# The mLSTM's norm factors and output scaling on GpSimd instead of VectorE and ScalarE, in a hybrid mLSTM and differential-attention block

## The chip, the cores and the metric

The kernel runs on one core of a Trainium2 chip. The metric is the device time of one execution in microseconds (us), given as the median of several runs. One further execution is recorded by the hardware profiler; all views quoted here come from it. The core's engines work side by side, each taking its own queue of instructions in order: TensorE (PE in the profile; PEld is its weight load), VectorE (DVE), ScalarE (ACT), GpSimd (POOL) and SyncE (SP, which here mostly issues DMAs).

## What is computed

One layer over a sequence of 1024 tokens with a model width of 1024, all in fp32. The input is normalised and projected by `w_in`; one part goes through a bidirectional mLSTM with 4 heads of 256 channels, another through differential attention with 8 heads; both branches are gated, mixed and projected out. The change touches the end of the mLSTM branch, the RMS norm of each head's output:

```python
def rmsnorm(x, g):
    xf = x.astype(jnp.float32)
    y = xf * lax.rsqrt(jnp.mean(xf * xf, axis=-1, keepdims=True) + NORM_EPS)
    return (y * g.astype(jnp.float32)).astype(x.dtype)
...
h_fw = mlstm_one_direction(mq, mk, mv, i_fw, lf_fw)
h_bw = flip(mlstm_one_direction(flip(mq), flip(mk), flip(mv), flip(i_bw), flip(lf_bw)))
hm = rmsnorm((h_fw + h_bw).transpose(0, 2, 1, 3), ml_norm_g[layer])
hm = hm.reshape(B, S, ML_WIDTH).astype(x.dtype)
y_a = hm * jax.nn.sigmoid(a_o) * jax.nn.silu(a_z)
```

For each token and head there is one norm factor, `rsqrt(mean(h*h) + eps)`, and the 256 outputs of that token and head are multiplied by it.

## The kernel before

The kernel passes through stages one after the other: normalising and transposing the input, projections and convolutions, differential attention (about 460 to 1110 us of the span), the mLSTM (about 1145 to 1390 us), then the mixing of the branches and the output projection. Large products are split in a high and a low part (`H`, `L`) and computed as three fp32r products each. The high part is a cast on ScalarE, the low part a subtraction on VectorE or GpSimd.

The order of TensorE's instructions is written out by hand after the opening stage (`keep(E.PE)`, the `Weaver`, and `ml_units` for the mLSTM). For ScalarE, VectorE, GpSimd and SP, the framework's planner makes the order of each queue at compile time, from the program's order and its own estimate of durations: of the instructions that it holds to be ready, it takes the one that stands first in the program. On the chip every queue is then taken strictly in that order, and an instruction that waits holds up those behind it.

The mLSTM runs head by head, n = 0 to 3, in `ml_units` (L1239 on). A head's sequence is cut in 8 tiles of 128 tokens, `tt` = 0 to 7. The steps of a tile, all in `ml_head`:

- `scores` (S): TensorE makes the 256-wide score tile; for both directions GpSimd masks the decay terms (`affine_select`, L1136, output `W`), ScalarE takes the exponential (L1138), VectorE multiplies with the scores and sums (L1139).
- `t_tile` (I): TensorE multiplies with the running states; VectorE makes the denominators and their reciprocal `rr` (L1165 to L1174), ScalarE writes the first part of the output `hm` (L1179) and scales `W` (L1183), VectorE adds the second direction (L1185, L1188).
- `transposes` (T): TensorE transposes `W`, ScalarE casts it to `WH` (L1198), VectorE makes `WL`.
- `pv` (P): TensorE multiplies `W` with the values into `PO`; VectorE adds that to `hm` (L1209); ScalarE squares it and sums along the row into one column of `ssq` (L1210). After the last tile (`tt == 7`), the norm factors of the whole head, 128x8 numbers `rs`, come from `self.rsqrt` (L1212).

`rsqrt` (L133 to L152) is shared by several places. It makes `val` from `ssq` (L140), raises it to the power -0.5 on GpSimd (L147, always there), and improves that by one Newton step of four small instructions (L148 to L151). All but L147 run on VectorE, or on the engine given as `eng`; the attention stage gives GpSimd.

`scale` (L1214) multiplies two tiles of `hm` by their factors, in place, on ScalarE (L1216). Then `out` (O) transposes the 128x256 tiles on TensorE, and VectorE applies the gain and the gate `gA` (L1228) before a DMA writes the result to memory.

A head's last steps run inside the next head: at t = 0 of head n+1 come T and P of tile 7 of head n, and so the norm factors; at t = 1 the first four scalings, at t = 2 the last four and the first half of the output transposes; at t = 3 the second half. TensorE's gaps are filled with pieces of the next head's value projection (L451, `pj`), whose weights are cast by ScalarE (L204, `wH`) and split by GpSimd in eight pieces (L207, `wL`). After head 3 there is no next head: its factors, scalings and output transposes come at about 1376 to 1385 us, with gate projections (L429) around them.

In the profile's names, `rh_v`, `rh_y`, `rh_w` are the tiles of the mLSTM's `rsqrt`, `rb_*` those of the attention's; `kwH` and `kwL` are the weighted keys, `CH` and `CL` the split state. The opening stage has a power of its own for the input norm (L516, 128x1), followed by VectorE's scaling of the input `x` (L527).

Of the kernel before, what the change touches and what calls it, by code (L numbers as in the profile page):

```python
# [11 lines left out]
ALU = mybir.AluOpType  # L12
# [4 lines left out]
EPS = 1e-6  # L17
NH_A, DH = 4, 256
# [91 lines left out]
class Block:  # L110
# [917 lines left out]
    def ml_head(self, n, st):  # L1028


        v, a, p, q, w2 = self.v, self.a, self.p, self.q, self.w2
        gc = self.gc
        row = lambda c: n * NC + c
        loc = {}
# [167 lines left out]
        def pv(tt):  # L1202
            vH, vL = st["v", tt // NB]
            WH, WL = loc.pop(("WT", tt))
            pairs = [(x[:, i, :], y[:, i, 0:DH]) for x, y in ((WH, vH), (WH, vL), (WL, vH)) for i in range(NB)]
            o = self.bank("PO")[:, 0:DH]
            self.mm(o, pairs)
            h = st["h"][tt]
            v.tensor_tensor(out=h, in0=o, in1=h, op=ALU.add)  # L1209
            a.activation(out=o, in_=h, func=AF.Square, accum_out=st["ssq"][:, tt:tt + 1])  # L1210
            if tt == 7:
                loc["rs"] = self.rsqrt(w2, st["ssq"], 1.0 / DH, EPS, "rh")  # L1212

        def scale(t):  # L1214
            for t in (t, t + 1):
                a.mul(st["h"][t], st["h"][t], loc["rs"][:, t:t + 1])  # L1216

        def load_g(half):
            for i in range(2):
# [3 lines left out]
        def out(i, half):  # L1223
            ps = self.bank("T")
            for k in range(4):
# [8 lines left out]
                    v=self.v_units("av", n, vv, order=(3, 2, 1, 0)), weigh=step(weigh),  # L1234
                    state=lambda c, d: [do(state, c, d, i) for i in range(2)], split=step(split), S=step(scores),
                    I=step(t_tile), T=step(transposes), P=step(pv), scale=step(scale), g=step(load_g),
                    O=lambda half: [do(out, i, half) for i in range(2)])

# [402 lines left out]
```

## Time and profile before

| what | value |
|---|---|
| median of 3 runs | 1686.43 us (1686.1 to 1689.79) |
| the profiled execution, its own time | 1687.36 us |
| its span in the trace | 1685.6 us |
| norm factors: instructions L147 to L151 of `rh_*`, each | x4, once a head |
| L1216, scaling of `hm` on ScalarE, 128x256 | x32, 14.5 us, mean 503 ns |
| L147 of `rh_y` on GpSimd | x4, 6.6 us, mean 1649 ns |
| L1216, first and last start | 1210.5 and 1382.9 us |

How to read the views. A view of stretches gives for each stretch its bounds and length, then for PE, PEld, DVE, ACT and POOL the busy time and, in brackets, the number of instructions, then the granted TensorE clock, the DMA engines' busy share and the GB/s. A view of waits says who waited for whom: total us, times, longest. A view in order of time gives start, duration, engine, line, operation, output and inputs with the shape; in square brackets stand the engine's idle time before the instruction and what ended it. Neighbouring instructions of one kind are merged (x3). The groups by line add the busy time and the mean in ns. Matmuls are pipelined and their ends are modelled, so that two of them may overlap in such rows.

### The profile page before, as it was taken

What the parts mean: (1) busy time and instruction counts of PE and PEld (TensorE: products, weight loads), DVE (VectorE), ACT (ScalarE), POOL (GpSimd) and SP (SyncE); (2) the same over time, 40 slices, a digit from 0 to 9 for tenths busy, and PEclk for the clock granted to TensorE, in tenths of its full rate; (3) what the DMA queues carried; (4) which work ended last, traced back from release to release, by engine and by line L of the source; (5) the groups of instructions that cost most, each with busy time, mean ns of one, the idle gap of its engine ahead of it and who ended that gap; (6) DMA issues with size and microseconds to landing.
All of it is one profiled execution on the core that took longest, in us unless ns stands there. A gap on an engine that the chain in (4) does not pass through costs nothing. (4 is left out here: it accounts for less than half of the span.)

```text
span 1685.6 us, 25370 instructions
## 1 busy us (share of the span) xinstructions
PE 1645.8 (98%) x9431; PEld 1385.3 (82%) x9431; DVE 992.4 (59%) x1799; ACT 760.3 (45%) x1522; POOL 635.2 (38%) x712
## 2 busy tenths in 40 slices
PE   7999999999999999999999999999999999999998
PEld 5777887887877988898888888899999877888887
DVE  5778678675286766666666665325666754135533
ACT  7454555553255454444445445334655644122221
POOL 5767676655343334333451332122322412212000
PEclk9999999999999999999999999999999999999999
DMA  5334434434231213211322222166455337344222
GB/s 180 101 117 137 138 113 137 126 125 127 74 80 48 74 38 88 51 51 39 100 59 56 62 58 70 57 181 176 144 160 161 89 117 244 126 149 126 88 93 83
DMA packets 175630, 178.79 MB, mean 106 GB/s; under 512 B 12185, under 2 KB 135410, under 8 KB 175506
## 3 DMA queue, kind: packets, MB, share of 16 engines
q1 hardware_dynamic: 174594, 175.58, 34.8%
q8 instruction: 74, 1.21, 0.3%
q10 hardware_dynamic: 912, 1.59, 0.2%
q14 instruction: 50, 0.41, 0.1%
HBM read 114.11 MB, written 46.24 MB: 95 GB/s over the span
## 5 line engine op out<-in xcount | busy, mean ns | idle before, releaser
L429 PE MATMUL pj<-hH,wH 128*128 128x512 f32 x640 | 265.8, 415 | 3.3 <-ACT f L542 1.5
L429 PE MATMUL pj<-hH,wL 128*128 128x512 f32 x640 | 251.3, 393 | 1.8 <-POOL wL L207 1.8
L429 PE MATMUL pj<-hL,wH 128*128 128x512 f32 x640 | 250.1, 391 | 0.2 <-DVE hL L580 0.2
L209 POOL TENSOR_TENSOR wL<-raw,wH 128x1024 fp32r<-128x1024 f32 x41 | 99.7, 2432 | 278.0 <-ACT wH L204 268.3
L928 ACT ACTIVATE e<-S,nm 128x1024 f32<-128x1024 f32 x128 | 142.7, 1115 | 134.1 <-DVE nm L926 133.9
L948 DVE TENSOR_TENSOR pL<-T,pH 128x512 fp32r<-128x512 f32 x128 | 87.9, 688 | 117.4 <-ACT pH L947 116.7
L926 DVE TENSOR_REDUCE nm<-S 128x1 f32<-128x1024 f32 x128 | 150.5, 1217 | 10.1 <-PE S L923 9.3
L451 PE MATMUL pj<-wH,hH 128*128 128x256 f32 x512 | 149.9, 293 | 1.6 <-DVE vL L1035 1.4
L429 PEld LDWEIGHTS pj<-hH,wH 128*128 128x128 f32 x640 | 120.4, 188 | 37.7 <-issue 14.1
L451 PE MATMUL pj<-wL,hH 128*128 128x256 f32 x512 | 144.9, 283 | 1.4 <-POOL wL L207 1.4
L429 PEld LDWEIGHTS pj<-hH,wL 128*128 128x128 f32 x640 | 120.1, 188 | 30.2 <-POOL wL L207 3.4
L451 PE MATMUL pj<-wH,hL 128*128 128x256 f32 x512 | 144.5, 282 | 0.0
L429 PEld LDWEIGHTS pj<-hL,wH 128*128 128x128 f32 x640 | 120.7, 189 | 18.2 <-DVE hL L580 0.6
L429 PE MATMUL pj<-sl_yb,wH 128*128 128x512 f32 x384 | 118.9, 390 | 2.1 <-DVE sl_mb L1339 1.6
L947 ACT CAST pH<-T 128x512 fp32r<-128x512 f32 x128 | 74.7, 584 | 100.5 <-PE T L131 99.8
L204 ACT CAST wH<-raw 128x1024 fp32r<-128x1024 f32 x56 | 58.8, 1050 | 114.7 <-PE pj L429 75.8
L923 PE MATMUL S<-kst,qq 64*128 64x512 f32 x768 | 106.5, 408 | 0.0
L451 PEld LDWEIGHTS pj<-wH,hH 128*128 128x128 f32 x512 | 97.7, 191 | 6.8 <-issue 3.9
L451 PEld LDWEIGHTS pj<-wL,hH 128*128 128x128 f32 x512 | 97.5, 190 | 2.3 <-POOL wL L207 2.3
L451 PEld LDWEIGHTS pj<-wH,hL 128*128 128x128 f32 x512 | 97.7, 191 | 0.1
L934 DVE SCALAR_TENSOR_TENSOR e<-e,r,e 128x1024 f32<-128x1024 f32 x64 | 88.9, 1389 | 2.2
L923 PEld LDWEIGHTS S<-kst,qq 64*128 64x128 f32 x768 | 67.8, 184 | 26.2 <-issue 10.5
(358 smaller groups left out, 4101.4 us busy)
## 6 DMA issues: line engine op xcount, KB each, us to landing
raw<-in_w_in_dram SPq DMA_DIRECT2D x88, 512.0 KB, 3.9
kst<-hl SPq DMA_DIRECT2D x64, 128.0 KB, 2.4
qq<-hl SPq DMA_DIRECT2D x64, 128.0 KB, 2.4
x<-in_x_dram SPq DMA_DIRECT2D x8, 512.0 KB, 6.2
cak<-y SPq DMA_DIRECT2D x16, 256.0 KB, 2.3
cakH<-cin SPq DMA_DIRECT2D x16, 256.0 KB, 4.4
cakL<-tz SPq DMA_DIRECT2D x16, 256.0 KB, 4.1
gm<-oz SPq DMA_DIRECT2D x16, 256.0 KB, 2.8
```

The costliest lines, as they stand in the source:

```text
L204: self.a.copy(wH, raw)
L209: self.p.tensor_tensor(out=wL, in0=raw, in1=wHf, op=ALU.subtract)
L429: self.t.matmul(ps, lhsT=l[:, k, :], rhs=r, start=(n == 0), stop=(n == 23))
L451: self.t.matmul(ps[:, i, :], lhsT=l, rhs=r[:, k, :], start=(kh == 0 and k == 0 and m == 0), stop=(kh == 1 and k == 3 and m == 2))
L923: self.t.matmul(ps[:, o], lhsT=qq[r, x, c], rhs=k[r, y, o], start=(m == 0), stop=(m == 2))
L926: v.tensor_reduce(out=nm, in_=ps, axis=AX.X, op=ALU.max, negate=True)
L928: a.activation(out=e, in_=ps, func=AF.Exp, bias=nm[:, 0:1], accum_out=Z[:, j, t:t + 1])
L934: v.scalar_tensor_tensor(out=e0, in0=e, scalar=r[:, 0:1], in1=e0, op0=ALU.mult, op1=ALU.add)
L947: a.copy(pH[:, :, s], ps)
L948: v.tensor_tensor(out=pL[:, :, s], in0=ps, in1=pH[:, :, s].bitcast(F32), op=ALU.subtract)
```

## The change

In `pv`, the norm factors' `rsqrt` gets `eng=p`, so that all its instructions run on GpSimd, for all four heads. In `scale`, heads 0, 1 and 2 (`n + 1 < NH_A`) multiply with a `tensor_scalar` on GpSimd, the factor being one number per partition; head 3 keeps ScalarE.

```diff
             if tt == 7:
-                loc["rs"] = self.rsqrt(w2, st["ssq"], 1.0 / DH, EPS, "rh")
+                loc["rs"] = self.rsqrt(w2, st["ssq"], 1.0 / DH, EPS, "rh", eng=p)
 
         def scale(t):
             for t in (t, t + 1):
-                a.mul(st["h"][t], st["h"][t], loc["rs"][:, t:t + 1])
+                if n + 1 < NH_A:
+                    p.tensor_scalar(out=st["h"][t], in0=st["h"][t], scalar1=loc["rs"][:, t:t + 1], scalar2=None, op0=ALU.mult)
+                else:
+                    a.mul(st["h"][t], st["h"][t], loc["rs"][:, t:t + 1])
```

## The prediction

> **What bounds the kernel now.** The page comes first, then the view of stretches (busy time per engine) over the mLSTM stage, from about 1145 to 1390 us, cut where one head hands over to the next: 0 to 1, 1 to 2, 2 to 3.
>
> ```profile
> PE 1645.8 (98%) x9431; PEld 1385.3 (82%) x9431; DVE 992.4 (59%) x1799; ACT 760.3 (45%) x1522; POOL 635.2 (38%) x712
> ```
> ```profile
> 1208.00:1218.00 10.00, 8.70 (x66) 7.69 (x65) 6.01 (x23) 7.61 (x21) 1.98 (x3) 1.00 0.53 171
> 1269.50:1279.50 10.00, 8.73 (x66) 7.72 (x66) 6.01 (x23) 7.63 (x21) 1.99 (x3) 1.00 0.53 170
> 1329.00:1339.00 10.00, 8.20 (x54) 6.98 (x53) 7.03 (x28) 7.75 (x22) 3.36 (x5) 1.00 0.20 54
> ```
>
> TensorE (PE) is busy 98% of the span, and its clock column stands at 1.00 in these stretches. So a change on other engines is worth only the idle time of TensorE that it takes away, here 10 minus busy: 1.30, 1.27 and 1.80 us. That ScalarE (ACT, 7.6 to 7.8 of 10) gets emptier is worth nothing by itself. GpSimd (POOL) is the emptiest. Next, who holds TensorE up: the view of waits, then the order of time of ScalarE and TensorE at 0 to 1.
>
> ```profile
> ACT hm L1216 <- DVE rh_y L151: 6.7, 3, 2.4
> ```
> ```profile
> 1210.49 1.31 ACT L1216 ACTIVATE hm<-hm,rh_y 128x256 f32<-128x256 f32 x3 [2.40 <-DVE rh_y L151]
> 1211.71 0.35 ACT L1198 CAST WH<-T 128x256 fp32r<-128x256 f32 x1
> ```
> ```profile
> 1212.11 0.51 PE L127 MATMUL PO<-vH,WH 128*128 128x256 f32 x2 [0.29 <-ACT WH L1198]
> ...
> 1213.64 0.38 PE L127 MATMUL T<-vH,kwH 128*128 128x258 f32 x1 [0.19 <-ACT kwH L1081]
> ...
> 1217.44 0.72 PE L131 MATMUL T<-ident,W 128*128 128x128 f32 x2 [0.75 <-ACT W L1183]
> ```
>
> Here the reader is to see a chain through ScalarE's queue. ScalarE stands 2.40 us at the first scaling (`hm`, L1216), because the norm factors (`rh_y`) are not there; then it does three scalings (1.31), and only then the cast `WH` that TensorE's product PO wants. TensorE waits three times, always for ScalarE: 0.29 + 0.19 + 0.75 = 1.23 of the 1.30. At 1 to 2 the idle time is 1.27 against 1.30, so I take the same picture. At 2 to 3 it is another engine:
>
> ```profile
> 1329.04 0.50 ACT L1183 ACTIVATE W<-W,rr 128x256 f32<-128x256 f32 x1
> ```
> ```profile
> 1330.76 0.17 DVE L148 TENSOR_TENSOR rh_w<-rh_y 128x8 f32<-128x8 f32 x1 [1.55 <-POOL rh_y L147]
> 1330.96 0.17 DVE L149 TENSOR_TENSOR rh_w<-rh_w,rh_v 128x8 f32<-128x8 f32 x1
> 1331.04 0.35 DVE L1185 SCALAR_TENSOR_TENSOR W<-W,rr,W 128x128 f32<-128x128 f32 x1
> ```
> ```profile
> 1331.44 0.44 PE L131 MATMUL T<-ident,W 128*128 128x128 f32 x2 [1.80 <-DVE W L1185]
> ```
>
> VectorE (DVE) stands 1.55 us at L148, which needs GpSimd's power (L147). Behind it in the queue is L1185, which has had its input since 1329.54 (1329.04 + 0.50), and TensorE waits 1.80 us for that one.
>
> **The change, part by part.** Removed from VectorE are five small instructions a head (L140, L148 to L151) with the wait at L148, and from ScalarE the 24 scalings of heads 0 to 2 with the wait for the factors. Added to GpSimd are the five small ones for four heads and 24 scalings; no DMA moves.
>
> *ScalarE at 0 to 1 and 1 to 2.* Without L1216 in the queue, `WH` can follow its transposes at once, and so can the work behind it. TensorE's waits of 0.29 and 0.19 go. The third (0.75) ends with L1183 on ScalarE, with VectorE's work behind it, which both move forward; it can stay in part, since VectorE takes its queue in order. Bounds: 0.48 (first two alone) and 1.30 (all the idle time). I take 1.2 each: all three name ScalarE.
>
> *VectorE at 2 to 3.* L1185 no longer stands behind L148. It can run at 1329.55, takes 0.35, and TensorE starts at about 1329.95 instead of 1331.44: 1.5 us. Below stands what could block it: bounds 0 and 1.8.
>
> *The factors on GpSimd.* The same recipe runs there already in the attention stage, in order of time:
>
> ```profile
> 546.18 0.24 POOL L145 TENSOR_SCALAR rb_v<-ms 128x8 f32<-128x8 f32 x1
> ...
> 546.78 1.67 POOL L147 TENSOR_TENSOR rb_y<-rb_v,mhalf 128x8 f32<-128x8 f32 x1
> ...
> 549.38 0.20 POOL L151 TENSOR_TENSOR rb_y<-rb_y,rb_w 128x8 f32<-128x8 f32 x1
> ```
> ```profile
> 1207.80 1.67 POOL L147 TENSOR_TENSOR rh_y<-rh_v,mhalf 128x8 f32<-128x8 f32 x1
> 1209.43 0.40 POOL L1136 TENSOR_SCALAR_AFFINE_SELECT W<-gb 128x256 f32<-128x256 f32 x1
> 1217.84 1.40 POOL L1136 TENSOR_SCALAR_AFFINE_SELECT W<-gb 128x128 f32<-128x128 f32 x2 [8.02 <-DVE W L1185]
> ```
>
> From the start of the power to the end of L151 are 549.58 - 546.78 = 2.80 us. At 0 to 1 that gives factors at 1207.9 + 2.8, about 1210.7, where ScalarE used them at 1210.49: no gain, no loss that matters. The reader is to see the hole after that: from 1209.83 to 1217.84 GpSimd has nothing to do.
>
> *The scalings on GpSimd.* No row shows GpSimd multiplying 128x256 by one number per partition. The groups by line (last columns: busy us, mean ns) give the nearest:
>
> ```profile
> L207 POOL TENSOR_TENSOR wL<-raw,wH 128x128 fp32r<-128x128 f32 x120 | 55.2, 496 | 35.3 <-ACT wH L204 33.2 <-POOL W L1136 2.0
> ...
> L868 POOL CAST hl<-m 128x512 fp32r<-128x512 f32 x32 | 25.3, 799 | 0.8
> ...
> L981 POOL TENSOR_TENSOR zg<-att,zg 128x512 f32<-128x512 f32 x16 | 20.6, 1288 | 76.6 <-ACT att L961 51.8 <-DVE zg L881 24.7
> ```
>
> Low end: half the cast of 128x512, 0.40, which is also the mask L1136 of 128x256 above. High end: a two-input instruction of that size, on the line through 0.496 (128 elements) and 1.288 (512): 0.76. The scaling has one tensor input, like cast and mask, so I take 0.45. Eight are 3.6 us; with some 1.1 for the small ones (2.80 - 1.67) they fill 4.7 of the 8.0 us of the hole. That hole hides them, at nothing. If an instruction of GpSimd holds its queue (masks L1136 wait for VectorE's L1185), the scalings behind it come late, and output transposes of the finished head wait; between the factors and the masks at 1217.84 I see room enough.
>
> *The last head* stays on ScalarE; only its factors move.
>
> ```profile
> 1376.74 1.65 POOL L147 TENSOR_TENSOR rh_y<-rh_v,mhalf 128x8 f32<-128x8 f32 x1 [10.22 <-DVE rh_v L140]
> 1378.35 3.37 POOL L207 TENSOR_TENSOR wL<-raw,wH 128x128 fp32r<-128x128 f32 x8
> ```
> ```profile
> 1380.12 3.31 ACT L1216 ACTIVATE hm<-hm,rh_y 128x256 f32<-128x256 f32 x8 [1.91 <-DVE rh_y L151]
> ```
>
> With 2.80 from the power they are ready at about 1379.65, 0.4 earlier than 1380.12, if GpSimd runs the small instructions before the split of a weight (`wL`, 3.37 us). The split then ends 1.2 us later; nothing shows TensorE waiting for it there, and if it did, that is the cost.
>
> *Sum.* 1.2 + 1.2 + 1.5 + 0.4 = 4.3 us. The profiled execution took 1687.36 us with a span of 1685.6, so it would take 1683.1 with a span of 1681.3. The median shown, 1686.43, is 0.93 below that execution: forecast 1682.1.
>
> *What can block L1185.* GpSimd and VectorE get in each other's way, and these rows of the opening show how for a power of 128x1:
>
> ```profile
> 22.25 0.55 POOL L516 TENSOR_TENSOR rsy<-rsv,mhalf 128x1 f32<-128x1 f32 x1 [6.23 <-DVE rsv L515]
> ...
> 28.89 1.05 POOL L516 TENSOR_TENSOR rsy<-rsv,mhalf 128x1 f32<-128x1 f32 x1 [0.98 <-DVE rsv L522]
> ```
> ```profile
> 29.09 0.81 DVE L527 TENSOR_SCALAR x<-x,rsy,rsv 128x1024 f32<-128x1024 f32 x1
> ```
>
> VectorE began at 29.09, inside a power begun at 28.89, and ended at 29.90; the power ended at 29.94, 1.05 long instead of 0.55. So there the power did not keep VectorE out, it was itself kept waiting. At 2 to 3 the power (about 1329.4) and L1185 (1329.55) meet in the same way, so I count L1185 as free. The Trainium skill, in SBUF — State Buffer, section "Who interferes with whom", states that a VectorE instruction with two SBUF inputs and a GpSimd instruction that reads SBUF share an interface, and that the first to start keeps it for the whole instruction. By that L1185 would stand until the power ends and the sum would be 2.8; the rows above speak against it for a power.
>
> **The rivals.**
> 1. *The power blocks L1185.* If a power of 128x8 keeps VectorE out for its 1.65 us, L1185 runs at about 1331.05, as now. For it: it is eight times wider than the one seen. Against: the rows above. Sum 4.3 - 1.5 = 2.8: 1683.6.
> 2. *The split goes first in the last head.* The planner may put the 3.37 us of `wL` between the power and the small instructions. The factors come 3.0 us later than now instead of 0.4 earlier. For it: the split already follows the power directly. Against: the split belongs to later work. Sum 4.3 - 0.4 - 3.0 = 0.9: 1685.5.
> 3. *GpSimd becomes the bound; slower.* At 0.76 each, and each held some 0.25 behind VectorE (an estimate: half of such a 0.45 scaling), eight scalings are 8.1 us; with 1.1 that is 9.2 against the hole of 8.0. The masks of 1217.84 then start 1.2 late, and with them the exponentials, VectorE's products and TensorE. It decides from (8.0 - 1.1) / 8 = 0.86 us for one scaling, waits included. At three handovers, with the gains lost: 1686.4 + 3.6 = 1690.0. Masks put behind scalings by the planner work the same way, earlier. Against: cast and mask are far under 0.86.
> 4. *It does not do what it says.* The planner's new order keeps ScalarE or VectorE waiting elsewhere, so that TensorE's gaps only move: about 1686.4.
>
> **How the numbers follow.** About 0.2% (3.4 us) is what a measurement of this kernel can tell from no change: faster is below 1683.1. Forecast 0.46, its own range 1680.9 (all idle time gone at the handovers, and the last head) to 1683.1. Rival 1: 0.16, rival 2: 0.10, rival 4: 0.06, all within 0.2%. Rival 3: 0.22, slower. So faster 0.46, same 0.32, slower 0.22. The range goes from 1680.0, since the profile's modelled ends make TensorE's gaps a little short, to 1689.5, most of rival 3 in it.
>
> **What would show it.** Right: no L1216 on ScalarE before 1370; `WH` at 0 to 1 soon after its transposes; TensorE's idle time in the three stretches below 0.3 each; at 2 to 3 no wait of TensorE for L1185 near 1.8; GpSimd scalings near 0.45, in one run after the factors. Wrong: a scaling of 0.6 or more; L1185 with a duration of over 1 us beside the power; masks that start later than now; the split between power and small instructions in the last head; new waits of TensorE for `hm`.

## The result, and the profile after

The changed kernel takes 1705.76 us (median of 4 runs, 1705.2 to 1706.58), the kernel before 1688.11 (4 runs, 1686.1 to 1690.31): a ratio of 1.0106, 95% interval 1.0093 to 1.0118. It is slower by some 18 us, where 1682.1 was forecast. The profiled execution has a span of 1703.4 us, 17.8 more than before.

GpSimd's busy time rose by 24 us (from 635.2), and ScalarE's fell by 7 (from 760.3); TensorE is still busy nearly throughout. The first row of the page after:

```profile
PE 1652.2 (97%) x9431; PEld 1392.0 (82%) x9431; DVE 988.4 (58%) x1779; ACT 753.0 (44%) x1498; POOL 659.5 (39%) x756
```

So the sum of busy times doesn't say where 18 us went; the stretches do. Here the span is cut at the same instructions in both kernels: the first weight cast of ScalarE (L204) in heads 0, 1 and 2, and the first gate activation `gt` (L837) after the last head. First before, then after (columns: bounds, length, busy time of PE, PEld, DVE, ACT, POOL, clock, DMA share, GB/s):

```profile
1196.19:1257.70 61.51, 59.25 (x482) 57.31 (x481) 40.46 (x147) 36.40 (x91) 15.91 (x41) 1.00 0.53 156
1257.70:1319.22 61.52, 59.28 (x482) 57.35 (x481) 40.49 (x147) 36.39 (x92) 15.91 (x41) 1.00 0.49 146
1319.22:1386.54 67.32, 61.03 (x393) 52.48 (x392) 43.10 (x154) 39.51 (x100) 22.54 (x48) 1.00 0.29 95
1386.54:1685.60 299.06, 289.71 (x1296) 239.43 (x1294) 113.84 (x185) 73.38 (x112) 44.15 (x24) 0.99 0.40 132
```
```profile
1195.61:1263.08 67.47, 60.49 (x482) 59.09 (x481) 39.45 (x142) 33.72 (x83) 23.52 (x54) 0.95 0.46 141
1263.08:1330.84 67.76, 60.87 (x482) 59.49 (x481) 39.52 (x142) 33.67 (x84) 23.36 (x54) 0.95 0.46 134
1330.84:1402.12 71.28, 62.98 (x393) 54.02 (x392) 40.90 (x144) 37.31 (x92) 31.69 (x66) 0.98 0.25 78
1402.12:1703.40 301.28, 291.40 (x1296) 240.57 (x1294) 113.74 (x185) 73.14 (x112) 44.20 (x24) 0.99 0.40 133
```

The four lengths grew by 5.96, 6.24, 3.96 and 2.22 us; less 0.58 that the kernel was ahead at the first cut, that is the 17.8. In the first two rows TensorE's idle time (length minus busy) went from 2.26 to 6.98 and from 2.24 to 6.89. Its busy time grew too, by 1.24 and 1.59 for the same 482 matmuls, and the clock column fell from 1.00 to 0.95.

Now the handover 0 to 1 in order of time: GpSimd, ScalarE, then TensorE's longest waits at all three handovers.

```profile
1207.44 1.67 POOL L147 TENSOR_TENSOR rh_y<-rh_v,mhalf 128x8 f32<-128x8 f32 x1
...
1210.04 0.20 POOL L151 TENSOR_TENSOR rh_y<-rh_y,rh_w 128x8 f32<-128x8 f32 x1
1210.34 6.35 POOL L1217 TENSOR_SCALAR hm<-hm,rh_y 128x256 f32<-128x256 f32 x7
1216.64 0.40 POOL L1136 TENSOR_SCALAR_AFFINE_SELECT W<-gb 128x256 f32<-128x256 f32 x1
```
```profile
1208.68 0.37 ACT L1198 CAST WH<-T 128x256 fp32r<-128x256 f32 x1 [1.16 <-PE T L131]
1217.08 0.51 ACT L1138 ACTIVATE W<-W,gc_negM 128x256 f32<-128x256 f32 x1 [8.03 <-POOL W L1136]
1217.49 0.46 ACT L1081 ACTIVATE kwH<-T,gc_ws 128x256 fp32r<-128x256 f32 x1
```
```profile
1218.00 0.58 PE L127 MATMUL T<-vH,kwH 128*128 128x258 f32 x1 [6.04 <-ACT kwH L1081]
...
1285.35 0.58 PE L127 MATMUL T<-vH,kwH 128*128 128x258 f32 x1 [6.02 <-ACT kwH L1081]
...
1341.51 0.44 PE L131 MATMUL T<-ident,W 128*128 128x128 f32 x2 [0.29 <-DVE W L1185]
...
1347.69 0.36 PE L127 MATMUL T<-vH,kwH 128*128 128x258 f32 x1 [3.17 <-POOL hm L1217]
```

Read it from the end. TensorE waits 6.04 us for the weighted keys `kwH`. In ScalarE's list `kwH` stands behind an exponential (L1138), which waits 8.03 us for a mask of GpSimd. In GpSimd's list that 256-wide mask stands behind seven scalings in a row, 6.35 us. Before, this mask ran at 1209.43, directly behind the power; the hole from 1209.83 in which the prediction put the scalings lay behind the mask, and the planner put them in front of it. `WH`, the cast that the change was to bring forward, did come forward, from 1211.71 to 1208.68. At 2 to 3 it is the same with three scalings: the 128-wide mask behind them starts at 1346.46, ScalarE has waited 4.43 us for it, and `kwH` ends at 1347.55, so that all but 0.1 of the 3.17 us that the profile puts down to `hm` is this chain.

What the gap does to TensorE's clock shows in short stretches around it (columns as above):

```profile
1212.00:1214.00 2.00, 0.00 (x0) 0.00 (x0) 0.00 (x0) 0.00 (x0) 2.00 (x4) 1.00 0.74 229
1214.00:1216.00 2.00, 0.00 (x0) 0.00 (x0) 0.00 (x0) 0.00 (x0) 2.00 (x3) 0.88 0.10 33
1216.00:1218.00 2.00, 0.00 (x1) 0.00 (x1) 0.02 (x1) 0.87 (x2) 1.95 (x3) 0.50 0.00 0
1218.00:1220.00 2.00, 2.00 (x7) 1.74 (x8) 1.46 (x4) 1.47 (x3) 0.00 (x0) 0.50 0.00 0
...
1222.00:1224.00 2.00, 2.00 (x18) 2.00 (x17) 1.93 (x9) 1.87 (x5) 0.63 (x2) 0.91 0.03 8
```

For two of these stretches all engines but GpSimd stand still. Some 3.6 us into the gap, which began at 1211.96, the granted clock halves (the 0.88 of 1214 to 1216 puts it at about 1215.5), and it is back only at about 1222.4 (the 0.91), so that TensorE works at half speed for some 4 us after the gap has ended at 1218.00. The Trainium skill, in TensorE: Matmul & The Clock Gate, section "What's actually happening", says that an idle window of about 3.4 us lowers the clock to 4/8 and a busy one restores it; these rows agree.

Last, the price, in the groups by line:

```profile
L1217 POOL TENSOR_SCALAR hm<-hm,rh_y 128x256 f32<-128x256 f32 x24 | 22.0, 934 | 0.3
```

A scaling takes 0.92 to 0.93 us (median and mean), twice the 0.45 taken and above the upper bound of 0.76.

### The profile page after: what moved, and what is told of

Same layout as the page of the kernel before. It is cut to its first block, busy times and chain, and to the rows that moved or that the text cites. A ratio compares the mean times of both kernels' runs of the same rounds, so it can differ in the third digit from the quotient of the medians.

```text
span 1703.4 us, 25388 instructions
## 1 busy us (share of the span) xinstructions
PE 1652.2 (97%) x9431; PEld 1392.0 (82%) x9431; DVE 988.4 (58%) x1779; ACT 753.0 (44%) x1498; POOL 659.5 (39%) x756
## 3 DMA queue, kind: packets, MB, share of 16 engines
q10 hardware_dynamic: 912, 1.59, 0.2%
## 5 line engine op out<-in xcount | busy, mean ns | idle before, releaser
L204 ACT CAST wH<-raw 128x1024 fp32r<-128x1024 f32 x56 | 58.8, 1050 | 114.6 <-PE pj L429 75.3
```

Source lines behind the costliest of these rows:

```text
L204: self.a.copy(wH, raw)
```

## The experiments

Two theories stood against each other. **Order**: what costs is that the scalings stand ahead of a mask on which the exponential and `kwH` wait. **Price**: GpSimd simply has 22 us more to do, wherever it stands. Ratios are to the kernel before on the same chip, with the 95% interval.

### The parts of the change, one at a time

Factors on GpSimd, all scalings on ScalarE:

```diff
-                if n + 1 < NH_A:
-                    p.tensor_scalar(out=st["h"][t], in0=st["h"][t], scalar1=loc["rs"][:, t:t + 1], scalar2=None, op0=ALU.mult)
-                else:
-                    a.mul(st["h"][t], st["h"][t], loc["rs"][:, t:t + 1])
+                a.mul(st["h"][t], st["h"][t], loc["rs"][:, t:t + 1])
```

> Only the norm factors move to GpSimd; all scalings stay on ScalarE. Theory (the scalings of 0.92 us on GpSimd, put by the planner ahead of the mask of tile 2, make the loss): the loss is gone, time 1682 to 1688, no TensorE wait over 2 us at a handover, and at 2 to 3 TensorE's wait of 1.80 us for L1185 shrinks since VectorE no longer stands at L148. Rival (the factors on GpSimd hold up GpSimd's queue, or VectorE through the shared interface): most of the 17.6 us stays, 1698 or more.

Measured: 1690.1 us, ratio 1.0012 (1.0003 to 1.0021). The waits of TensorE from 1200 to 1345 us:

```profile
PE PO L127 <- ACT WH L1198: 3.4, 4, 1.1
...
PE T L131 <- DVE W L1185: 0.3, 1, 0.3
```

Most of the loss is gone, though the time is 2 us above the range expected. The wait for L1185 has shrunk as forecast, from 1.80 to 0.3, but TensorE now waits up to 1.1 us for `WH` at each handover: at 0 to 1 the factors come half a us later than in the kernel before (1211.00 against 1210.49), and ScalarE does four scalings ahead of `WH` instead of three. After these short waits the clock dips as well, to 0.62 and 0.52 in the stretches 1336 to 1338 and 1338 to 1340. The factors alone gain nothing.

Scalings on GpSimd, factors on VectorE:

```diff
-                loc["rs"] = self.rsqrt(w2, st["ssq"], 1.0 / DH, EPS, "rh", eng=p)
+                loc["rs"] = self.rsqrt(w2, st["ssq"], 1.0 / DH, EPS, "rh")
```

> Only the scalings of heads 0 to 2 move; the factors stay with VectorE as before. Theory: scalings again 0.92 us, TensorE gaps of 3 to 6 us at each handover, time 1700 to 1708. Rival (factors make the loss): 1684 to 1690.

Measured: 1697.42 us, ratio 1.0055 (1.0041 to 1.007), between the two expectations. Five scalings stand ahead of the mask here and not seven, and the waits for `kwH` are 3.7 us each:

```profile
1211.10 4.56 POOL L1217 TENSOR_SCALAR hm<-hm,rh_y 128x256 f32<-128x256 f32 x5 [0.91 <-DVE rh_y L151]
1215.61 0.41 POOL L1136 TENSOR_SCALAR_AFFINE_SELECT W<-gb 128x256 f32<-128x256 f32 x1
```

So the scalings are the part that costs. Scalings on VectorE, with the factors on GpSimd:

```diff
-                    p.tensor_scalar(out=st["h"][t], in0=st["h"][t], scalar1=loc["rs"][:, t:t + 1], scalar2=None, op0=ALU.mult)
+                    v.tensor_scalar(out=st["h"][t], in0=st["h"][t], scalar1=loc["rs"][:, t:t + 1], scalar2=None, op0=ALU.mult)
```

> The changed kernel with the 24 scalings on VectorE instead of GpSimd, the factors on GpSimd. VectorE's scaling of 128x1024 by two numbers per partition takes 0.81 us in the opening, so 128x256 should take about 0.3 us. Theory: ScalarE is free of them as was meant, GpSimd's masks are on time, 1681 to 1686. Rival (VectorE's queue takes ScalarE's place: scalings wait there for the factors in front of L1185 or the casts' low parts): 1686 to 1692 with TensorE waiting for VectorE at the handovers.

Measured: 1692.62 us, ratio 1.0021 (1.0011 to 1.0031), 0.344 us for one. VectorE in order of time at 0 to 1:

```profile
1211.76 2.30 DVE L1217 TENSOR_SCALAR hm<-hm,rh_y 128x256 f32<-128x256 f32 x8 [3.02 <-POOL rh_y L151]
1213.98 0.41 DVE L1035 TENSOR_TENSOR WL<-T,WH 128x256 fp32r<-128x256 f32 x1
```

The same thing on another engine: all eight scalings stand together ahead of `WL`, which TensorE waits for (1.2 us). At 2 to 3 TensorE waits longer, though a single scaling stands in the way. It waits for the factors in VectorE's queue, with L1185 behind it, as L148 did before the change:

```profile
1334.29 0.35 DVE L1217 TENSOR_SCALAR hm<-hm,rh_y 128x256 f32<-128x256 f32 x1 [3.03 <-POOL rh_y L151]
1334.56 0.34 DVE L1185 SCALAR_TENSOR_TENSOR W<-W,rr,W 128x128 f32<-128x128 f32 x1
```
```profile
1334.95 0.44 PE L131 MATMUL T<-ident,W 128*128 128x128 f32 x2 [3.13 <-DVE W L1185]
```

Behind this wait the clock dips too (0.53 and 0.62 in the stretches 1336 to 1338 and 1338 to 1340). So it is the rival that came about, 0.6 us above its range, and at 2 to 3 what costs is the wait for the factors and not the 0.34 us of a scaling.

### The price of a scaling

A fixed number, 0.25, in place of the factor; the outputs of heads 0 to 2 are not normalised:

```diff
-p.tensor_scalar(out=st["h"][t], in0=st["h"][t], scalar1=loc["rs"][:, t:t + 1], scalar2=None, op0=ALU.mult)
+p.tensor_scalar(out=st["h"][t], in0=st["h"][t], scalar1=0.25, scalar2=None, op0=ALU.mult)
```

> The changed kernel with the 24 GpSimd scalings multiplying by the fixed number 0.25 instead of the factor, so heads 0 to 2 are not normalised; they no longer wait for the factors. If the one-number-per-partition operand makes the price, the scaling takes 0.3 to 0.5 us, eight take under 4 us, and the time is 1681 to 1688. If 128x256 costs 0.92 us in any form, the gaps and some 1700 us stay.

Measured: 1694.5 us, ratio 1.0036 (1.0022 to 1.005); 0.855 us for one. Reading a factor per partition is only some 0.07 of the price. Since these scalings wait for no factors, they are spread over the head, one behind each tile. The price stayed, but not the 1700 us that were to go with it: with nearly the same work on GpSimd as in the changed kernel, the loss is a third of it. That speaks for order.

The same product with two tensor inputs:

```diff
-p.tensor_scalar(out=st["h"][t], in0=st["h"][t], scalar1=loc["rs"][:, t:t + 1], scalar2=None, op0=ALU.mult)
+p.tensor_tensor(out=st["h"][t], in0=st["h"][t], in1=loc["rs"][:, t:t + 1].broadcast_to([128, DH]), op=ALU.mult)
```

> The changed kernel, with the scaling on GpSimd written as a product of two tensors, the second one the factor broadcast along the row. Theory: the price of 0.92 us belongs to the form with a scalar operand; the two-input form stands at 0.70 to 0.80 us, interpolated from the kernel's own two-input rows on GpSimd; seven of them take some 5.3 instead of 6.35 us, TensorE's waits for kwH go from 6.0 to about 5 us, and the time is 1700 to 1704 us. Rival: it is the engine's price for any fp32 product of 256 elements, 0.92 us or more each, and the time is 1705 us or more.

Measured: 1699.74 us, ratio 1.0067 (1.0052 to 1.0082); 0.614 us for one, like the time a little below what was expected. GpSimd, then TensorE, at 0 to 1:

```profile
1211.01 4.04 POOL L1217 TENSOR_TENSOR hm<-hm,rh_y 128x256 f32<-128x256 f32 x7
1215.00 0.40 POOL L1136 TENSOR_SCALAR_AFFINE_SELECT W<-gb 128x256 f32<-128x256 f32 x1
```
```profile
1216.36 0.39 PE L127 MATMUL T<-vH,kwH 128*128 128x258 f32 x1 [3.73 <-ACT kwH L1081]
```

The row of seven is 2.31 us shorter (6.35 to 4.04), and the wait 2.31 shorter (6.04 to 3.73). Between these two kernels, whose order is the same, each us in that row is a us of TensorE.

A plain copy in the scaling's place, again without normalising heads 0 to 2:

```diff
-p.tensor_scalar(out=st["h"][t], in0=st["h"][t], scalar1=loc["rs"][:, t:t + 1], scalar2=None, op0=ALU.mult)
+p.tensor_copy(st["h"][t], st["h"][t])
```

> The changed kernel, with a plain copy in the place of each scaling on GpSimd; the outputs of heads 0 to 2 are not normalised. Theory 'price': a copy of 128x256 stands near 0.35 to 0.45 us, the price that the prediction took for a scaling; then the run of seven takes about 3 us instead of 6.35, TensorE's waits for kwH fall to 2 to 3 us, the clock stays whole, and the time is 1688 to 1695 us. By the prediction's own sum it would be 1682 us. Rival 'order': a mask behind seven instructions costs the handover whatever their length, waits of 5 us or more remain, and the time is over 1700 us.

Measured: 1692.28 us, ratio 1.0019 (1.001 to 1.0028); 0.398 us for one. No wait of TensorE for `kwH` above 0.4 us is left, but like e3 it needs no factors, and its copies are spread; so it gives the price of a copy and says nothing of seven in a row. As a test of the rival it missed.

### The order

A third buffer for `W1`, so that the mask of tile 2 needn't wait for one:

```diff
-                W = w2.tile([128, L], F32, name=f"W{d}", tag=f"W{d}", bufs=2)
+                W = w2.tile([128, L], F32, name=f"W{d}", tag=f"W{d}", bufs=2 + d)
```

> The changed kernel with a third buffer for W1, so that the 256-wide mask of a next head's tile no longer waits for its buffer until the first heads' scalings stand in GpSimd's list. Theory 'order' (what costs is that seven scalings of 0.92 us run ahead of that mask, and ScalarE's list holds kwH behind the mask's exponential): the mask runs ahead of most scalings, TensorE's waits of 6.0 us for kwH at the first two handovers shrink below 3 us, the halved clock behind them goes, and the time is 1686 to 1696 us. Rival 'price' (24 scalings of 0.92 us on GpSimd cost this wherever they stand): the waits move to another mask or to the output product, and the time stays at 1700 us or more. Second rival, the order of the list doesn't move with the buffer: 1704 to 1707 us and the same waits.

Measured: 1712.56 us, ratio 1.0138 (1.0122 to 1.0153), slower than the change itself and outside every expectation. GpSimd, then ScalarE:

```profile
1214.01 6.36 POOL L1217 TENSOR_SCALAR hm<-hm,rh_y 128x256 f32<-128x256 f32 x7
1220.33 0.29 POOL L1136 TENSOR_SCALAR_AFFINE_SELECT W<-gb 128x128 f32<-128x128 f32 x1
```
```profile
1220.65 0.40 ACT L1138 ACTIVATE W<-W,gc_negM 128x128 f32<-128x128 f32 x1 [7.59 <-POOL W L1136]
1220.96 0.46 ACT L1081 ACTIVATE kwH<-T,gc_ws 128x256 fp32r<-128x256 f32 x1
```

The 256-wide mask did move ahead, but now the next tile's 128-wide mask stands behind the seven, and ScalarE's list has that tile's exponential ahead of `kwH`. The buffer moved the place, not the trouble: TensorE still waits 5.5 and 5.8 us for `kwH`. Two waits of up to 1.6 us for the weight cast `wH` (L204) are new; what else makes this kernel slower than the change stays open.

Then the order itself, with the price left at 0.92. GpSimd is held to the program's order for a part of each head (`order[0]` begins that, `order[1]` ends it), and in the program the scalings come behind the scores:

```diff
+            self.order = (keep(E.PE, E.Pool), keep(E.PE))
...
-                if prev and t in (1, 2):
-                    un += prev["scale"](4 * t - 4)
...
                 if t < 7:
-                    un += x["S"](t + 1)
+                    un += [self.order[0]] * (t == 1 and prev is not None) + x["S"](t + 1)
...
                 if prev and t in (1, 2):
-                    un += prev["scale"](4 * t - 2)
+                    un += prev["scale"](4 * t - 4) + prev["scale"](4 * t - 2) + [self.order[1]] * (t == 2)
```

> The changed kernel, with GpSimd held to the program's order from t = 1 to t = 2 of each head, and the scalings put behind the scores' masks there: the 256-wide mask of tile 2 first, then four scalings, then the masks of tile 3, then four. The price of a scaling stays at 0.92 us, 24 of them, all on GpSimd. Theory 'order' (what cost 16 us is where the scalings stand, ahead of the mask that the exponential and kwH wait behind): TensorE's waits of 6.0 us for kwH and of 3.2 us for hm are gone (below 1 us each), its clock stays whole at the handovers, and what is left is the handovers' gain of up to 3.9 us against a tail longer by 2.2: 1685 to 1692 us. Rival 'price' (22 us more work on GpSimd cost this wherever they stand): the masks of tile 3 are late in place of those of tile 2, waits of 3 us or more remain, and the time is 1697 us or more.

Measured: 1686.5 us (10 runs, 1684.51 to 1689.16), ratio 0.9988 (0.9979 to 0.9997). GpSimd at 0 to 1, then the same four stretches as above:

```profile
1210.67 0.40 POOL L1136 TENSOR_SCALAR_AFFINE_SELECT W<-gb 128x256 f32<-128x256 f32 x1
1211.06 3.66 POOL L1217 TENSOR_SCALAR hm<-hm,rh_y 128x256 f32<-128x256 f32 x4
1217.24 1.21 POOL L1136 TENSOR_SCALAR_AFFINE_SELECT W<-gb 128x256 f32<-128x256 f32 x2 [2.52 <-PE T L131]
1218.43 3.79 POOL L1217 TENSOR_SCALAR hm<-hm,rh_y 128x256 f32<-128x256 f32 x4
```
```profile
1196.09:1256.62 60.53, 59.08 (x482) 57.29 (x481) 39.57 (x142) 33.44 (x84) 24.03 (x54) 1.00 0.53 158
1256.62:1316.97 60.35, 59.10 (x482) 57.35 (x481) 39.83 (x142) 33.55 (x83) 23.67 (x54) 1.00 0.49 149
1316.97:1384.38 67.41, 62.08 (x393) 52.84 (x392) 40.44 (x144) 36.68 (x92) 32.19 (x66) 1.00 0.27 83
1384.38:1683.70 299.32, 290.02 (x1296) 239.34 (x1294) 114.12 (x185) 73.12 (x112) 44.21 (x24) 0.99 0.41 134
```

GpSimd is as busy as in the changed kernel (24.03 against 23.52 in the first stretch), and yet the whole loss is gone, with the clock at 1.00 throughout. Price as a cause of its own has fallen: the 24 scalings of 0.92 us cost nothing that the time shows where they stand now.

Two edits were made there. The second alone, the scalings behind the scores in the program with GpSimd's list left to the planner:

> The changed kernel, with the scalings put behind the scores' masks in the program as in e13_order, but GpSimd's list left to the planner. Theory (it is the planner that takes ready scalings ahead of a mask that it doesn't hold to be ready, wherever they stand in the program): seven scalings stand ahead of the mask as in the changed kernel, waits of 6 us, 1704 to 1707 us. Rival (the place in the program was enough): 1685 to 1690 us.

Measured: 1705.59 us, ratio 1.0105 (1.0091 to 1.0119). The planner again puts seven in front of the mask:

```profile
1210.65 6.36 POOL L1217 TENSOR_SCALAR hm<-hm,rh_y 128x256 f32<-128x256 f32 x7
1216.97 0.40 POOL L1136 TENSOR_SCALAR_AFFINE_SELECT W<-gb 128x256 f32<-128x256 f32 x1
```

And the first alone, in the kernel before (the hold from t = 1 to t = 2, nothing of the change):

> The kernel before, with GpSimd held to the program's order from t = 1 to t = 2 of each head and nothing else. Theory (the gain of e13_order is the change's own, from ScalarE's and VectorE's handovers): GpSimd's list hardly differs from that of before, ratio 0.9994 to 1.0006. Rival (the hold itself is what gains): ratio as in e13_order, 0.998 to 0.9993.

Measured: 1687.81 us, ratio 0.9998 (0.999 to 1.0007): the hold by itself does nothing that can be measured. The kernel of e13 was run once more beside these:

> The kernel of e13_order once more, as the yardstick for the three beside it, on the same chip: 0.9979 to 0.9997 of the kernel before, as there.

Measured: 1687.26 us, ratio 0.9999 (0.9991 to 1.0008). The removal of the loss repeats; the gain of 0.12% over the kernel before doesn't.

### The last head, and versions that might beat both

In the changed kernel the stretch from `gt` to the end of the span is 2.22 us longer. With the last head's factors on GpSimd the last split (L207) ends later, and with it the load of the next weights that reuses its buffer: it is issued at 1399.02, 3.10 us ahead of `gt`; before, it was 4.79 ahead (1381.75 and 1386.54). Putting only the last head's factors back:

```diff
-                loc["rs"] = self.rsqrt(w2, st["ssq"], 1.0 / DH, EPS, "rh", eng=p)
+                loc["rs"] = self.rsqrt(w2, st["ssq"], 1.0 / DH, EPS, "rh", eng=p if n + 1 < NH_A else None)
```

> The changed kernel, with the factors of the last head made on VectorE and ScalarE as before, and those of heads 0 to 2 on GpSimd. Theory: the later end of the last head's split brings the load of the branch weights from 4.8 to 3.1 us ahead of gt and into the loads of yraw, and so lengthens the stretch from gt to the end of the span from 299.1 to 301.3 us; here the load stands 4.7 to 4.8 us ahead of gt again, the stretch is 299.0 to 299.4 us, the gain of 0.4 us in the last head is lost, and the time is 1.3 to 2.3 us below the changed kernel's, 1703.4 to 1704.5 us. Rival: the 2.2 us of the tail are an accident of the clock or of the loads' phase, the stretch stays at 300.5 to 302, and the time at 1705 us or more.

Measured: 1705.82 us, ratio 1.0101 (1.0084 to 1.0118), no different from the change. In its profile the load is back at 4.80 us ahead of `gt`, and the stretch at 298.78 us (1702.9 - 1404.12), but from the first cut to `gt` it took 1.5 us longer, of which the 0.4 us of the last head's factors had been expected. The same edit on e1:

> Only the factors of heads 0, 1 and 2 on GpSimd; all scalings on ScalarE and the last head's factors as before the change. e1_factors_only stood at 1.0012 of the kernel before, with a tail of 302.5 instead of 299.1 us. Theory: the last head's factors alone cost it that; here the tail is 298.8 to 299.4 us and the time 2.0 to 3.4 us below that run's ratio, 0.998 to 1.000 of the kernel before. Rival: factors on GpSimd give nothing at the handovers and what the tail gives back is scatter: ratio 1.000 to 1.002.

Measured: 1690.96 us, ratio 1.0013 (1.0004 to 1.0022), as e1. And on e13:

> As e13_order, with the last head's factors made on VectorE and ScalarE as before the change. Theory (the later load of the branch weights costs the tail something even without a halved clock): the load stands 4.8 us ahead of gt again, and the time is 0.3 to 1.0 us below e13's, beyond the 0.4 us lost in the last head. Rival (the tail of one profiled execution is scatter): no difference from e13's, or up to 0.5 us above it.

Measured: 1686.22 us, ratio 0.9989 (0.998 to 0.9998), beside e13b's 0.9999. Over all profiles, the stretch is 298.13 to 299.83 us where the load stands 4.8 ahead (8 kernels), and 299.32 to 302.47 where it stands 3.1 ahead (10 kernels). The means of the two groups are 299.0 and 300.7, so that the later load may well lengthen the stretch. But of the three pairs that differ in it alone, two show no difference in the ratio, and in the third (e13b and e15, 1.0 us) the intervals overlap: it stays open.

With the order held, the two-input form and the last head's factors as before:

> As e13_order, with the scaling written with two tensor inputs (0.61 us in place of 0.92 each) and the factors of the last head made on VectorE as before the change. It is meant as a version that could beat both. Theory: order costs nothing then, the tail is back at 298.8 to 299.4 us, and the handovers' gain stays in part: 1684.5 to 1688 us, 1 to 4 us below the kernel before. Rival: something behind the scalings (tile 3's masks, output transposes, the split of weights) is late in its turn, and the time is 1688 to 1693 us, not below the kernel before.

Measured: 1687.08 us, ratio 0.9989 (0.9981 to 0.9998). The cheaper form brings nothing over e15: off the path its price doesn't matter. Only two of eight scalings on GpSimd (tiles 6 and 7 of heads 0 to 2, two-input form), list left to the planner, last head's factors as before:

```diff
-                if n + 1 < NH_A:
+                if n + 1 < NH_A and t >= 6:
```

> Factors of heads 0 to 2 on GpSimd, of the last head as before the change; of each of the first three heads only the scalings of tiles 6 and 7 on GpSimd, with two tensor inputs (0.61 us each), the other six on ScalarE. Theory (the mask of tile 2 stands behind whatever scalings are ready when it isn't): it now stands behind two, 1.2 us, and not seven, 6.35; the mask starts about as early as in the kernel before, TensorE's waits for kwH are below 1 us, and the time is 0.998 to 1.001 of the kernel before. Rival: ScalarE's six scalings still wait for the factors ahead of WH, TensorE waits 1 us for WH at each handover as in e1_factors_only, and the ratio is 1.001 to 1.003.

Measured: 1690.84 us, ratio 1.0014 (1.0005 to 1.0023). The wait for `kwH` is below 0.4 us with two in front of the mask, but TensorE waits 1.1 us for `WH` as in e1: the rival held.

So of the four runs that have the change, or most of it, with the order held (e13, e13b, e14, e15), three are some 0.1% below the kernel before, and one is not: a gain there is at most of that size.

## Why the prediction was wrong, by its own steps

**The step that failed** is "That hole hides them, at nothing", in the part on the scalings. The hole from 1209.83 to 1217.84 was there, but it began behind a mask that itself stood behind the power. The prediction compared lengths (4.7 us into 8.0) and did not ask what stands ahead of the hole in GpSimd's list. The planner took the scalings first, seven of them, and ScalarE's list carried the delay on from the mask by the exponential to `kwH`, for which TensorE waited 6.0 us at each of two handovers. The experiments e13 and c2 differ only in who makes GpSimd's order, and stand at 1686.5 and 1705.59 us.

**The price** failed too, 0.92 for 0.45, outside the bounds of 0.40 to 0.76. It made a wrong place dear, but it wasn't the cause: with the place right, 0.92 costs nothing (e13), and with it wrong, 0.45 would not have saved the forecast. By the slope of e6, a row of 7 x 0.45 = 3.15 us would leave a wait of 6.04 - (6.35 - 3.15) = 2.8 us, an estimate that no run here checks. The argument for 0.45 was that the scaling has one tensor input like a cast and a mask. The copy, of the same shape, does cost 0.398; the one-input product doesn't, and the two-input one (0.614) is cheaper than that.

**Rival 3** had the right sign and named the mechanism in half a sentence ("Masks put behind scalings by the planner work the same way, earlier"), but priced it at the far end of the hole, as if only the masks of 1217.84 could be late: 1.2 us a handover and 0.86 us for a scaling as the point from which it decides. In front of the first mask that point lies far lower: a row of 6.35 us cost a wait of 6.04, one of 4.04 a wait of 3.73, so beyond the first 0.3 us each scaling costs its whole length.

**Rival 4** (the new order keeps ScalarE waiting elsewhere) came nearest to the mechanism, since it is ScalarE that stands 8.03 us at L1138, but it was priced at no change. Three of the signs named for being wrong came: a scaling of over 0.6 us, masks that start later, a new wait put down to `hm`.

**Rival 2** fell: in the last head the small instructions ran from 1394.62 to 1395.67, ahead of the split.

**The clock** was in no step. The two waits of 6 us halved it, and the same matmuls took 1.24 and 1.59 us longer in the first two stretches. With the idle time that makes the 6 us of a handover: 4.72 + 1.24 = 5.96 at 0 to 1.

**What held.** ScalarE at 0 to 1 and 1 to 2: 1.2 us each were forecast; with the order right, e13 shows 61.51 - 60.53 = 0.98 and 61.52 - 60.35 = 1.17, and its second profile (e13b) 1.05 and 1.05. Some 0.26 of each stands in the profile of c1 too, which has nothing of the change. The factors on GpSimd: 2.80 us from the power's start to the end of L151, measured 1210.24 - 1207.44 = 2.80. The last head: 0.4 us forecast; from one `gt` to the next it went from 9.01 to 8.61 (1393.51 to 1402.12). L1185 at 2 to 3: TensorE's wait for it fell from 1.80 to 0.29, and rival 1 fell with it, as VectorE's row at 2 to 3 shows beside GpSimd's:

```profile
1341.10 0.35 DVE L1185 SCALAR_TENSOR_TENSOR W<-W,rr,W 128x128 f32<-128x128 f32 x1 [0.45 <-ACT W L1183]
```
```profile
1340.87 1.67 POOL L147 TENSOR_TENSOR rh_y<-rh_v,mhalf 128x8 f32<-128x8 f32 x1
```

L1185, with two inputs in SBUF, ran from 1341.10 to 1341.45, inside the power (1340.87 to 1342.54), at its usual length. The Trainium skill, in SBUF — State Buffer, section "Who interferes with whom", calls the pair of ports that the two engines share an exclusive lock, and has the first keep it for its whole instruction (this it says of VectorE's two-port modes). By that L1185 would have stood until 1342.54; for this power that does not hold.

**What held as a wait but not as time.** The 1.5 us of L1185 did not become time: in e13 the stretch from head 2 to `gt` is 67.41 against 67.32 us, though the last head's 0.4 is in it. TensorE waits up to 0.9 us for `WH` there instead; its idle time did fall, from 6.29 to 5.33, but the same 393 matmuls show 1.05 us more of busy time at a full clock. Why, no run here shows. So even with its order right, the change was worth less than half of the 4.3 us: the spans of its two profiles are 1683.7 (e13) and 1686.4 (e13b) against 1685.6, and in the medians it is between nothing and 0.1%.

**Later split.** "Nothing shows TensorE waiting for it": the split did delay a load, as told above; whether that costs time is open.

**A bound added up wrong.** All idle time gone at the handovers, and the last head, are 1.30 + 1.27 + 1.80 + 0.4 = 4.77 us. From the median of 1686.43 that is 1681.7; the 1680.9 of the prediction comes out only from the span of 1685.6 (1680.8). Nothing else hangs on it.

## What to carry to other kernels

Before new work is put into an engine's hole, list what stands in its queue between the moment at which the work becomes ready and the start of the hole: a planner that takes whatever is ready may put it in front of all of that, and then it can cost nearly its whole length on the path, whatever the engine's share of busy time. Follow each instruction so delayed to the in-order list of the engine that consumes it, since the wait is paid by what stands behind it there. Where the order is the cause, it can be tested at an unchanged price by holding that queue to the program's order.

## What the runs showed of the hardware

- On GpSimd, 128x256 in fp32: a product with a scalar operand 0.92 us (with a fixed number 0.855), a product of two tensors, the second the factor broadcast along the row, 0.614, a plain copy 0.398, a mask 0.40. The same scalar product is 0.344 on VectorE, and a scaling on ScalarE was 0.503. The Trainium skill, in GPSIMD Engine Reference, section "Engine selection", has two-input elementwise work about twice as slow as on VectorE and one-input work roughly at line rate. The copy fits that (VectorE's copy of 128x258 at L1103, which reads PSUM, takes 0.42); the one-input product, 2.7 times VectorE's, does not; the two-input product is 1.5 times VectorE's sum at L1209 (0.42, one input in PSUM).
- In the two gaps of 6 us TensorE's granted clock halved after some 3.6 and 4.5 us, and it stayed halved for some 4.3 and 5.3 us after work had begun again. In these two stretches the same matmuls took 1.2 and 1.6 us longer.
- A gap shorter than that can be followed by the same: after the wait of 3.17 us at 2 to 3 the clock column shows 0.66 and 0.50 in the stretches 1348 to 1350 and 1350 to 1352, when work had begun again, and in e1 three waits of 0.29, 1.10 and 0.25 us within 6 us were enough. In the kernel before, the wait of 1.80 us at 2 to 3 left the clock at 1.00. How long a wait has to be, these runs do not show.
